# A tile's transposes between the halves of the tile before, and the input scaled on GpSimd: the first unit of a hybrid RG-LRU / mLSTM layer

## The chip, the cores and the metric

The kernel runs on one core of one Trainium2 chip. The metric is the time of one execution in device microseconds; the time of a kernel is the median of several runs. The engines are named as in the profile: PE (TensorE, the matrix products; PEld is its loading of weights), DVE (VectorE), ACT (ScalarE), POOL (GpSimd, which also issues the stores), SP (SyncE, which issues the loads).

## The reference, cut to what matters

One layer of a decoder trunk is computed for 1024 prompt tokens and for 8 single decode tokens. The part that the change touches is its start: a row-wise normalisation of the input and one wide input projection.

```
def rmsnorm(x, g):
    y = x * lax.rsqrt(jnp.mean(x * x, axis=-1, keepdims=True) + EPS)
    return y * g
...
hn = rmsnorm(x, g_norm)                 # x: 1024 tokens x 1024
u = hn @ w_in                           # 1024 x 7176
xa, za, uq, uk, uv, uo, zb, ui, uf = jnp.split(u, SPLIT_IDX, axis=-1)
...                                     # RG-LRU on xa, mLSTM on q, k, v, two gates, merge
x = x + merged @ w_out
y = rmsnorm(x, g_final)
```

The eight gate columns ui and uf are the last 8 of the 7176.

## The kernel before, in words

**Units.** The projection is done in 14 units of 512 columns (two blocks of 256). Units 1 to 13 use seven block products in place of eight (a Strassen-like scheme): they need the turned, normalised input and five sums and differences of its quarters, kept in SBUF as seven pairs cb_hi[q], cb_lo[q]. Every operand is split into a rounded high part and the low rest, and a product is the sum of three: high x high, high x low, low x high (mm3, L64 to L66). A split (L70, L71) is one cast on ACT (hi) and one subtraction on DVE (lo).

**The first unit** (v0 and v1, with the eight gate columns beside v0) is different: it does the plain product tile by tile of 128 tokens while the input arrives, and builds the seven pairs on the way. The change lies here. For each tile, in the order xorder = 4, 0, 8, 5, 1, 6, 2, 7, 3 (8 is the tile of the 8 decode tokens), the steps are:

- x_fetch (L366): load 128 x 1024 of x from SP's queue into a buffer of the pool ws, which has six and also holds the four tiles of split v1 weights w1h, w1l.
- x_stats (L371, L181 to L189): ACT squares the tile and sums it (tile junk), then the square root on ACT (L185) and four small steps on DVE give the factor in st.
- x_turn (L382, L386): one DVE operation multiplies x by the factor and by g_norm (gn_b); eight PE transposes put the turned tile into two PSUM banks (two of ps_kv, or ps_s and ps_qp, in turn).
- x_split (L70, L71): the two halves are cast and subtracted into b12h, b12l (tiles 4 to 7, first half) or into cb_hi, cb_lo.
- plain (L64 to L66): two halves of 24 products each, the first with the v0 weights and gates (wph, wpl), the second with the v1 weights (w1h, w1l), into ps_o, of which there are three banks. Each result is copied out by ACT (pe, L461) and stored by POOL (d_v, L464).
- x_copy and x_combos (L408, L420, L424 to L426): the sums and differences, each split again.

Ahead of the first tile 17 products of ones (L469) run on PE. Behind the last tile in the text come the gate product of the decode tokens (L510, bias added into gd, L512), the decode product of the first unit (dec_unit, L228: hnd against the raw weights) and the loads of the next unit's raw weights (raw_1, L215).

**What sets the order.** The text gives dependences and a priority; a scheduler places the instructions on each engine, and each engine then runs its queue in that order. So the order below is the built program's and not the text's.

Of the kernel before, what the change touches and what calls it, by code (L numbers as in the profile page):

```python
# [17 lines left out]
P = 128  # L18
T = 1024
HT = 512  # L20
NB = 8
KC = 8
# [27 lines left out]
def hymba_kernel(  # L50
# [7 lines left out]
    V, A, G, TE = nc.vector, nc.scalar, nc.gpsimd, nc.tensor  # L58
    ld = nc.sync.dma_start
    stq = nc.gpsimd.dma_start  # L60

    def mm3(out, ah, al, bh, bl, first, last):

        TE.matmul(out, ah, bh, start=first, stop=False, skip_group_check=True)  # L64
        TE.matmul(out, ah, bl, start=False, stop=False, skip_group_check=True)  # L65
        TE.matmul(out, al, bh, start=False, stop=last, skip_group_check=True)  # L66

    def split(hi, lo, src):

        A.copy(hi, src)  # L70
        V.tensor_tensor(lo, src, hi.bitcast(F32), op=ALU.subtract)  # L71
# [9 lines left out]
    def ps(tag, shape):  # L81
        return psp.tile(shape, F32, tag=tag, name=f"ps_{tag}", bufs=NBUF.get(tag, 1))
# [121 lines left out]
    raws = {}  # L204
# [18 lines left out]
    def dec_unit(u):  # L223

        pz = ps("tr", [P, 512])
        for k in range(KC):
            g = k % 4
            TE.matmul(pz[32 * g:32 * g + 32, :], hnd[:, k, :], raws[u, k // 4][:, k % 4, :], start=k < 4, stop=k >= 4,  # L228
                      skip_group_check=True)
# [12 lines left out]
        late.append(turn)  # L242
# [114 lines left out]
    es_f = ExitStack()  # L357
    fp = es_f.enter_context(tc.tile_pool(name="f_start", bufs=1))
    gn_b = fp.tile([P, T], F32, tag="gn_b", name="gn_b")
    xorder = [4, 0, 8, 5, 1, 6, 2, 7, 3]  # L360
    rows_of = lambda i: P if i < 8 else NB
    xt, xps, bf = {}, {}, {}

    def x_fetch(i):
        xt[i] = ws([P, T], f"x{i}", F32)
        ld(xt[i][:rows_of(i)], x_prompt[0, i * P:(i + 1) * P, :] if i < 8 else x_sample[:, 0, :])  # L366

    def x_stats(i):
        n = rows_of(i)
        junk = fp.tile([P, T], BF16, tag="junk", name="junk")  # L370
        A.activation(junk[:n], xt[i][:n], AF.Square, accum_out=st0[:n, i, 0:1])  # L371
        rsqrt_mean(st0[:n, i, 1:2], st0[:n, i, 0:1], st0[:n, i, 2:3], T)

    def x_turn(m):
        i = xorder[m]
        n = rows_of(i)
        xps[i] = []
        for half in range(2):
            hs = slice(half * HT, (half + 1) * HT)
            if m == 0 or half == 0:  # L380
                s = hs if m == 0 else slice(0, T)
                V.scalar_tensor_tensor(xt[i][:n, s], xt[i][:n, s], st0[:n, i, 1:2], gn_b[:n, s], op0=ALU.mult, op1=ALU.mult)  # L382
            pt = ps(("kv", "kv", "s", "qp")[(2 * m + half) % 4], [P, 4, P])
            for q in range(4):
                k = half * 4 + q
                TE.transpose(pt[:, q, 0:n], xt[i][:n, k * P:(k + 1) * P], idF[:n, :n])  # L386
            xps[i].append(pt)
        del xt[i]

    def x_split(i, half):  # L390

        p = xps[i][half]
        if i == 8:
            V.tensor_copy(hnd[:, 4 * half:4 * half + 4, 0:NB], p[:, :, 0:NB])
            return
        s = slice(i % 4 * P, (i % 4 + 1) * P)
        if i >= 4 and half == 0:
            bf[i] = [fp.tile([P, 4, P], F32R, tag=f"b12{n}", name=f"b12{n}") for n in "hl"]
            split(*bf[i], p)
        else:  # L400
            q = Q_P3 if i >= 4 else (Q_P1, Q_P2)[half]
            split(cb[q][0][:, :, s], cb[q][1][:, :, s], p)
# [33 lines left out]
    def w1_split(b):  # L436

        t = ws([P, 4, 256], f"w1h{b}"), ws([P, 4, 256], f"w1l{b}")
        split(t[0], t[1], raws[0, b][:, :, 256:512])
        w1.append(t)  # L440

    gs = dconst([P, NCH, 8], "gs")

    def plain(i):

        s = slice(i % 4 * P, (i % 4 + 1) * P)
        op = []
        for k in range(KC):
            if i < 4:
                op.append([t[:, k % 4, s] for t in cb[Q_P1 if k < 4 else Q_P2]])  # L450
            elif k < 4:
                op.append([t[:, k, :] for t in bf[i]])
            else:
                op.append([t[:, k % 4, s] for t in cb[Q_P3]])
        for w in range(2):
            pt = ps("o", [P, 512])[:, 0:264 - 8 * w]
            for k, (h, l) in enumerate(op):
                wh, wl = (hi[:, k, :], lo[:, k, :]) if w == 0 else (t[:, k % 4, :] for t in w1[k // 4])
                mm3(pt, h, l, wh, wl, k == 0, k == KC - 1)
            t = fp.tile([P, 256], F32, tag="pe", name="pe", bufs=2)  # L460
            A.copy(t, pt[:, 0:256])  # L461
            if w == 0:
                V.tensor_tensor(gs[:, i, :], pt[:, 256:264], bgate, op=ALU.add)
            stq(d_v[w][i * P:(i + 1) * P, :], t)  # L464

    pw = ps("tr", [P, P])

    for _ in range(17):
        TE.matmul(pw, ones, ones, start=True, stop=True)  # L469
    x_fetch(xorder[0])  # L470
    ld(gn_b, g_norm[0].partition_broadcast(P))
    load_raw(0, 0, (0,))
    ld(wg, w_in[0, :, C_G:C_G + 8].rearrange("(k p) c -> p k c", p=P))
    load_raw(0, 1, (0,))
    x_fetch(xorder[1])
    load_raw(0, 0, (1,))
    load_raw(0, 1, (1,))
    ld(bgate[:, 0:4], b_mi[0].partition_broadcast(P))
    ld(bgate[:, 4:8], b_mf[0].partition_broadcast(P))
    x_stats(xorder[0])  # L480
    x_stats(xorder[1])
    for m, i in enumerate(xorder):
        x_turn(m)
        if m == 0:
            def w0_split(k):
                split(hi[:, k:k + 2, 0:256], lo[:, k:k + 2, 0:256], raws[0, k // 4][:, k % 4:k % 4 + 2, 0:256])
            w0_split(0)
            split(hi[:, :, 256:264], lo[:, :, 256:264], wg)
            x_split(i, 0)
            w0_split(2)  # L490
            x_split(i, 1)
            w0_split(4)
            w0_split(6)
            for b in range(2):
                w1_split(b)
        else:
            x_split(i, 0)
            x_split(i, 1)
        if 4 <= i < 8:
            x_copy(i)  # L500
        if m + 2 < 9:
            x_fetch(xorder[m + 2])
            x_stats(xorder[m + 2])
        if i < 8:
            plain(i)
            x_combos(i)

    pgd = ps("tr", [32, 8])
    for k in range(KC):
        TE.matmul(pgd, hnd[:, k, :], wg[:, k, :], start=k == 0, stop=k == KC - 1)  # L510
    gd = dconst([NB, 8], "gd")
    V.tensor_tensor(gd, pgd[0:NB], bgate[0:NB], op=ALU.add)  # L512
    ld(d_gd, gd)
    dec_unit(0)
    load_raw(1, 0)
    load_raw(1, 1)
    es_f.close()


# [1021 lines left out]
```

## Time and profile before

| what | value |
|---|---|
| median of 3 runs | 948.93 us (947.85 to 950.67) |
| the profiled execution | 948.28 us, its span 946.5 us |
| PE busy | 927.4 us, 98% of the span |
| DVE, ACT, POOL busy | 75%, 62%, 15% |
| chain that ended last | PE 89%, DVE 5%, DMA 2%, ACT 2% |
| from the first product of the first unit to the first of the next | 9.80 to 79.24 us |

A row of the timeline reads: start, duration, engine, line, operation, output<-inputs, partitions x elements, and in brackets the idle time just before with what ended it. A row of the waits reads: who waited, for whom, total us, times, longest. PE's durations are those of a pipeline: products follow each other faster than one of them lasts, so work is read from start to start.

### The profile page before, as it was taken

To read this page: it belongs to the slowest core of one execution; us is meant where nothing else is said; L and a number is where in the kernel's file an instruction comes from. 1 tells how busy PE (TensorE), PEld (TensorE's weight loads), DVE (VectorE), ACT (ScalarE), POOL (GpSimd) and SP (SyncE) were. 2 spreads that over 40 slices of the span, in tenths; PEclk is the share of its full clock that TensorE was granted. 3 is DMA by queue.
4 is the path that set the end of the run, shared out by engine and by line. 5 is a ranking of instruction groups with operands and counts; after the bars stand their busy time and mean duration, and the time that the engine had idled before them with its cause. 6 is when DMAs were issued, how large, how long until landed. Compare 5 with 4: busy or idle time off the path is not lost.

```text
span 946.5 us, 15380 instructions
## 1 busy us (share of the span) xinstructions
PE 927.4 (98%) x5355; PEld 763.1 (81%) x5355; DVE 711.1 (75%) x1488; ACT 583.2 (62%) x1041; POOL 144.6 (15%) x254
## 2 busy tenths in 40 slices
PE   7999999999999999999999999999999999999996
PEld 7887778777787887777789898877687888888886
DVE  5876787889788788798877966678766777677663
ACT  5563446777677666768667684457646456456542
POOL 1110111121202131112112212010200100000110
PEclk9999999999999999999999999999999999999999
DMA  5431455275636564437645545436873664465431
GB/s 183 151 128 37 142 176 183 81 242 187 221 116 223 178 219 150 150 112 264 202 152 180 201 134 166 129 106 228 305 210 116 177 187 121 137 187 152 128 85 51
DMA packets 131251, 153.69 MB, mean 162 GB/s; under 512 B 15658, under 2 KB 109930, under 8 KB 131166
## 3 DMA queue, kind: packets, MB, share of 16 engines
q1 hardware_dynamic: 113446, 96.84, 34.5%
q0 software_dynamic: 17728, 55.87, 16.2%
q8 instruction: 42, 0.69, 0.3%
q14 instruction: 35, 0.29, 0.1%
HBM read 101.09 MB, written 51.65 MB: 161 GB/s over the span
## 4 chain that ended last, share of the span: by engine, by line
PE 89%; DVE 5%; DMA 2%; ACT 2%; issue 1%; SPq 0%; DVEq 0%; ACTq 0%
PE ps_o L64 14%; PE ps_o L66 14%; PE ps_o L65 14%; PE ps_kv L64 11%; PE ps_kv L65 10%; PE ps_kv L66 10%; PE ps_tr L228 3%; PE ps_s L746 2%; PE ps_s L1076 1%; PE ps_qp L910 1%; DMA raw<-in_w_in_dram 1%; PE ps_qp L64 1%; PE ps_tr L1213 1%; PE ps_qp L65 1%; PE ps_qp L66 1%
## 5 line engine op out<-in xcount | busy, mean ns | idle before, releaser
L70 ACT CAST wh<-raw 128x1024 fp32r<-128x1024 f32 x91 | 95.6, 1050 | 75.2 <-PE ps_o L65 30.3
L71 DVE TENSOR_TENSOR wl<-raw,wh 128x1024 fp32r<-128x1024 f32 x91 | 111.1, 1221 | 39.2 <-ACT wh L70 21.7
L64 PE MATMUL ps_kv<-cb_hi,wh 128*128 128x512 f32 x320 | 128.0, 400 | 0.7 <-ACT s L309 0.7
L66 PE MATMUL ps_kv<-cb_hi,wl 128*128 128x512 f32 x320 | 125.4, 392 | 0.0
L65 PE MATMUL ps_kv<-cb_lo,wh 128*128 128x512 f32 x320 | 125.1, 391 | 0.0
L64 PE MATMUL ps_o<-cb_hi,wh 128*128 128x512 f32 x240 | 94.8, 395 | 0.0
L66 PE MATMUL ps_o<-cb_hi,wl 128*128 128x512 f32 x240 | 93.7, 390 | 0.0
L65 PE MATMUL ps_o<-cb_lo,wh 128*128 128x512 f32 x240 | 93.6, 390 | 0.0
L64 PEld LDWEIGHTS ps_kv<-cb_hi,wh 128*128 128x128 f32 x320 | 60.1, 188 | 22.9 <-issue 5.5
L66 PEld LDWEIGHTS ps_kv<-cb_hi,wl 128*128 128x128 f32 x320 | 60.1, 188 | 13.1
L65 PEld LDWEIGHTS ps_kv<-cb_lo,wh 128*128 128x128 f32 x320 | 60.1, 188 | 11.8
L64 PE MATMUL ps_kv<-wh,cb_hi 128*128 128x256 f32 x192 | 55.1, 287 | 0.0
L65 PE MATMUL ps_kv<-wl,cb_hi 128*128 128x256 f32 x192 | 54.6, 284 | 0.0
L66 PE MATMUL ps_kv<-wh,cb_lo 128*128 128x256 f32 x192 | 54.5, 284 | 0.0
L64 PEld LDWEIGHTS ps_o<-cb_hi,wh 128*128 128x128 f32 x240 | 45.1, 188 | 11.6 <-issue 2.5
L64 PE MATMUL ps_o<-wo,mh 128*128 128x512 f32 (+1 forms) x136 | 53.2, 392 | 1.0 <-ACT mh L70 1.0
L66 PEld LDWEIGHTS ps_o<-cb_hi,wl 128*128 128x128 f32 x240 | 45.0, 188 | 9.8
L64 PE MATMUL ps_o<-wo,rh 128*128 128x512 f32 (+1 forms) x136 | 52.9, 389 | 0.0
L65 PEld LDWEIGHTS ps_o<-cb_lo,wh 128*128 128x128 f32 x240 | 45.1, 188 | 9.1
L66 PE MATMUL ps_o<-wo,rl 128*128 128x512 f32 (+1 forms) x136 | 51.8, 381 | 0.0
L65 PE MATMUL ps_o<-wo,rh 128*128 128x512 f32 (+1 forms) x136 | 51.7, 380 | 0.0
L65 PE MATMUL ps_o<-wo,mh 128*128 128x512 f32 (+1 forms) x136 | 51.6, 380 | 0.0
(469 smaller groups left out, 2524.9 us busy)
## 6 DMA issues: line engine op xcount, KB each, us to landing
raw<-in_w_in_dram SPq DMA_DIRECT2D x56, 512.0 KB
Cb<-in_state_mlstm_C_dram SPq DMA_DIRECT2D x32, 256.0 KB
out_dram<-Cb POOLq DMA_DIRECT2D x32, 256.0 KB, 4.1
qk<-d_qk SPq DMA_DIRECT2D x32, 256.0 KB
oraw<-in_w_out_dram SPq DMA_DIRECT2D x16, 512.0 KB
d_qk<-s POOLq DMA_DIRECT2D x24, 256.0 KB, 3.0
x<-in_x_prompt_dram SPq DMA_DIRECT2D x8, 512.0 KB
d_x<-s POOLq DMA_DIRECT2D x16, 256.0 KB, 2.5
```

Of the source, the lines that this page charges most:

```text
L64: TE.matmul(out, ah, bh, start=first, stop=False, skip_group_check=True)
L65: TE.matmul(out, ah, bl, start=False, stop=False, skip_group_check=True)
L66: TE.matmul(out, al, bh, start=False, stop=last, skip_group_check=True)
L70: A.copy(hi, src)
L71: V.tensor_tensor(lo, src, hi.bitcast(F32), op=ALU.subtract)
L228: TE.matmul(pz[32 * g:32 * g + 32, :], hnd[:, k, :], raws[u, k // 4][:, k % 4, :], start=k < 4, stop=k >= 4, skip_group_check=True)
L746: TE.matmul(pg, w[:, n, :], st["xx"][n], start=k == 0, stop=k == 1)
L910: TE.matmul(pq[32 * g:32 * g + n, 0:256], qsel[:, kb, 4 * bb:4 * bb + n], ds_["C", h * NB + bb][:, kb, :], start=b == 1, stop=b == NB - 1, ...
L1076: TE.matmul(S, qk[:, 2 + kb, :], qk[:, kb, :], start=kb == 0, stop=kb == 1)
L1213: TE.matmul(dec_o[0][32 * g:32 * g + 32, :], md, oraw[m][:, half * 512:(half + 1) * 512], start=first and m in ms[:2], stop=last and m in ...
```

## The change

All edits are in the first unit.

- The decode tile 8 leaves xorder; loads have an order of their own, xload, with the decode tile third. x_turn8 turns the decode tile into one bank ps_tr.
- x is scaled by two GpSimd operations in x_stats, a multiply by gn_b and a multiply by the factor, for all tiles but the first, which stays with DVE in x_turn. Every third tile loaded has a buffer x2 of its own; junk moves to the staging pool.
- plain does one half at a time, and its products are grouped by four: high x high, then low x high, then high x low (in the very first group high x low comes second). The next tile's transposes and splits stand between the two halves.
- The splits of the second weights and the statistics of the next tiles stand ahead of the first product; the copies b12f and b22f of the first tile stand behind its products.
- 19 and 4 products of ones instead of 17; the gate product, dec_unit(0) and the raw_1 loads stand behind the third tile.

Three places in the built programs. First PE, at the end of the first tile (x4, whose second half goes into ps_o_306 before and ps_o_338 now) and the transposes of the second tile, x0. Before:

```order
L66 MATMUL ps_o_306<-w1h1_259,cb_lo5_166 128x256
L386 MATMUL ps_s_339<-idF_78,x0_205 128x128 x4
L386 MATMUL ps_qp_344<-idF_78,x0_205 128x128 x4
L64 MATMUL ps_o_363<-wph_175,cb_hi0_155 128x264
L65 MATMUL ps_o_363<-wpl_176,cb_hi0_155 128x264
```

And now:

```order
L473 MATMUL ps_o_338<-w1h0_255,b12h_243 128x256 x4
L473 MATMUL ps_o_338<-w1h0_255,b12l_244 128x256 x2
L394 MATMUL ps_s_312<-idF_78,x0_207 128x128 x4
L394 MATMUL ps_qp_317<-idF_78,x0_207 128x128 x4
L473 MATMUL ps_o_338<-w1h0_255,b12l_244 128x256 x2
L473 MATMUL ps_o_338<-w1l0_256,b12h_243 128x256 x4
L473 MATMUL ps_o_338<-w1h1_269,cb_hi5_165 128x256 x4
L473 MATMUL ps_o_338<-w1h1_269,cb_lo5_166 128x256 x4
L473 MATMUL ps_o_338<-w1l1_270,cb_hi5_165 128x256 x4
L473 MATMUL ps_o_374<-wph_175,cb_hi0_155 128x264 x4
```

x0's transposes have moved from behind the tile's 48th product to behind its 30th; 18 products of the first tile now stand between them and the first product of x0. At x5 the transposes stand behind the 42nd product of x0, at x1 behind the 34th of x5, from x6 on behind the 24th.

Second POOL, from its last early instruction on (pe is the copied result of a half). Before, only stores are queued:

```order
L658 DMA out_8_dram<-in_state_rglru_conv_dram 8x2048
L464 DMA d_v0_129<-pe_302 128x256
L464 DMA d_v1_130<-pe_331 128x256
L464 DMA d_v0_129<-pe_388 128x256
L464 DMA d_v1_130<-pe_417 128x256
```

And now the two multiplies of each tile stand between the stores:

```order
L381 TENSOR_TENSOR x0_207<-x0_207,gn_b_174 128x1024
L479 DMA d_v0_129<-pe_308 128x256
L382 TENSOR_SCALAR x0_207<-x0_207,st0_117 128x1024
L381 TENSOR_TENSOR x8_213<-x8_213,gn_b_174 8x1024
L479 DMA d_v1_130<-pe_363 128x256
L382 TENSOR_SCALAR x8_213<-x8_213,st0_117 8x1024
L381 TENSOR_TENSOR x5_326<-x5_326,gn_b_174 128x1024
L479 DMA d_v0_129<-pe_399 128x256
L382 TENSOR_SCALAR x5_326<-x5_326,st0_117 128x1024
L381 TENSOR_TENSOR x1_429<-x1_429,gn_b_174 128x1024
L479 DMA d_v1_130<-pe_468 128x256
L381 TENSOR_TENSOR x6_441<-x6_441,gn_b_174 128x1024
```

A store that waits for the end of a half (pe) now holds back the second multiply of a tile, and a multiply holds back stores.

Third ACT, from the last cast of the v0 weights on. Before:

```order
L70 CAST wph_175<-raw1_0_203 128x2x256 x2
L408 COPY b12f_263<-ps_kv_228 128x512
L371 ACTIVATE junk_219,st0_117<-x0_205 128x1024
L408 COPY b22f_264<-ps_kv_234 128x512
L185 ACTIVATE st0_117<-st0_117 128x1
L70 CAST w1h0_255<-raw0_0_200 128x1024
L461 COPY pe_302<-ps_o_277 128x256
L70 CAST w1h1_259<-raw1_0_203 128x1024
```

And now:

```order
L70 CAST wph_175<-raw1_0_205 128x2x256 x2
L378 ACTIVATE junk_259,st0_117<-x0_207 128x1024
L185 ACTIVATE st0_117<-st0_117 128x1
L476 COPY pe_308<-ps_o_283 128x256
L70 CAST w1h0_255<-raw0_0_202 128x1024
L70 CAST w1h1_269<-raw1_0_205 128x1024
L70 CAST cb_hi0_155<-ps_s_312 128x4x128
```

The two copies of the first tile have left the place ahead of the second weights, and the copy pe of its first half, which stood behind the first of their casts, stands ahead of both.

The diff, cut to its core:

```diff
-    xorder = [4, 0, 8, 5, 1, 6, 2, 7, 3]
+    xorder = [4, 0, 5, 1, 6, 2, 7, 3]
+    xload = [4, 0, 8, 5, 1, 6, 2, 7, 3]
...
+    def x_fetch(n):
+        if n < len(xload):
+            i = xload[n]
+            xt[i] = fp.tile([P, T], F32, tag="x2", name=f"x{i}") if n % 3 == 2 else ws([P, T], f"x{i}", F32)
+            ld(xt[i][:rows_of(i)], x_prompt[0, i * P:(i + 1) * P, :] if i < 8 else x_sample[:, 0, :])
+    def x_stats(n, scale=True):
+        if n < len(xload):
+            i = xload[n]
+            r = rows_of(i)
+            junk = sg([P, T], "junk", BF16)
+            x = xt[i][:r]
+            A.activation(junk[:r], x, AF.Square, accum_out=st0[:r, i, 0:1])
+            rsqrt_mean(st0[:r, i, 1:2], st0[:r, i, 0:1], st0[:r, i, 2:3], T)
+            if scale:
+                G.tensor_tensor(x, x, gn_b[:r], op=ALU.mult)
+                G.tensor_scalar(x, x, st0[:r, i, 1:2], None, op0=ALU.mult)
...
-            if m == 0 or half == 0:
-                s = hs if m == 0 else slice(0, T)
-                V.scalar_tensor_tensor(xt[i][:n, s], xt[i][:n, s], st0[:n, i, 1:2], gn_b[:n, s], op0=ALU.mult, op1=ALU.mult)
+            if m == 0:
+                hs = slice(half * HT, (half + 1) * HT)
+                V.scalar_tensor_tensor(xt[i][:, hs], xt[i][:, hs], st0[:, i, 1:2], gn_b[:, hs], op0=ALU.mult, op1=ALU.mult)
...
+    def x_turn8():
+        pt = ps("tr", [P, KC, NB])
+        for k in range(KC):
+            TE.transpose(pt[:, k, :], xt[8][:NB, k * P:(k + 1) * P], idF[:NB, :NB])
+        V.tensor_copy(hnd[:, :, 0:0 + NB], pt)
+        del xt[8]
...
-    def plain(i):
+    def plain(i, w):
...
-        for w in range(2):
-            pt = ps("o", [P, 512])[:, 0:264 - 8 * w]
-            for k, (h, l) in enumerate(op):
-                wh, wl = (hi[:, k, :], lo[:, k, :]) if w == 0 else (t[:, k % 4, :] for t in w1[k // 4])
-                mm3(pt, h, l, wh, wl, k == 0, k == KC - 1)
+        pt = ps("o", [P, 512])[:, 0:264 - 8 * w]
+        for k0 in (0, 4):
+            terms = [(0, 0), (0, 1), (1, 0)] if w == 0 and i == xorder[0] and k0 == 0 else [(0, 0), (1, 0), (0, 1)]
+            for x, y in terms:
+                for k in range(k0, k0 + 4):
+                    wt = (hi, lo)[y][:, k, :] if w == 0 else w1[k // 4][y][:, k % 4, :]
+                    TE.matmul(pt, op[k][x], wt, start=k == 0 and (x, y) == (0, 0), stop=k == KC - 1 and (x, y) == terms[-1],
+                              skip_group_check=True)
...
-    for _ in range(17):
+    for _ in range(19):
...
+    x_fetch(2)
+    x_stats(0, False)
+    x_turn(0)
+    for _ in range(4):
+        TE.matmul(pw, ones, ones, start=True, stop=True)
...
+    w0_split(6)
+    w1_split(0)
+    x_stats(1)
+    w1_split(1)
+    x_stats(2)
     for m, i in enumerate(xorder):
+        plain(i, 0)
+        if m + 1 < 8:
+            x_turn(m + 1)
+            for half in range(2):
+                x_split(xorder[m + 1], half)
+        if m == 1:
+            x_turn8()
         if m == 0:
+            x_fetch(3)
+            x_stats(3)
+        elif m == 1:
+            x_fetch(4)
+            x_stats(4)
+            x_fetch(5)
+        plain(i, 1)
+        if i >= 4:
             x_copy(i)
+        x_combos(i)
+        if m == 1:
+            x_stats(5)
+        elif m > 1:
+            x_fetch(m + 4)
+            x_stats(m + 4)
+        if m == 2:
+            pgd = ps("tr", [32, 8])
...
+            dec_unit(0)
+            load_raw(1, 0)
+            load_raw(1, 1)
```

More of the change, by code (lines that the diff above doesn't have):

```diff
@@ L385, in x_turn @@
                 k = half * 4 + q
-                TE.transpose(pt[:, q, 0:n], xt[i][:n, k * P:(k + 1) * P], idF[:n, :n])
+                TE.transpose(pt[:, q, :], xt[i][:, k * P:(k + 1) * P], idF)
             xps[i].append(pt)
         del xt[i]
+    def x_turn8():
[4 more added lines that the diff above has]
+        del xt[8]
     def x_split(i, half):
         p = xps[i][half]
-        if i == 8:
-            V.tensor_copy(hnd[:, 4 * half:4 * half + 4, 0:NB], p[:, :, 0:NB])
-            return
         s = slice(i % 4 * P, (i % 4 + 1) * P)
@@ L454, in plain @@
                 op.append([t[:, k % 4, s] for t in cb[Q_P3]])
-        for w in range(2):
-            pt = ps("o", [P, 512])[:, 0:264 - 8 * w]
-            for k, (h, l) in enumerate(op):
-                wh, wl = (hi[:, k, :], lo[:, k, :]) if w == 0 else (t[:, k % 4, :] for t in w1[k // 4])
-                mm3(pt, h, l, wh, wl, k == 0, k == KC - 1)
[L460 to L464, printed above, removed]
+        pt = ps("o", [P, 512])[:, 0:264 - 8 * w]
[6 more added lines that the diff above has]
+                              skip_group_check=True)
+        t = fp.tile([P, 256], F32, tag="pe", name="pe", bufs=2)
+        A.copy(t, pt[:, 0:256])
+        if w == 0:
+            V.tensor_tensor(gs[:, i, :], pt[:, 256:264], bgate, op=ALU.add)
+        stq(d_v[w][i * P:(i + 1) * P, :], t)
     pw = ps("tr", [P, P])
-    for _ in range(17):
+    for _ in range(19):
         TE.matmul(pw, ones, ones, start=True, stop=True)
-    x_fetch(xorder[0])
+    x_fetch(0)
     ld(gn_b, g_norm[0].partition_broadcast(P))
@@ L474, in hymba_kernel @@
     load_raw(0, 1, (0,))
-    x_fetch(xorder[1])
+    x_fetch(1)
     load_raw(0, 0, (1,))
@@ L479, in hymba_kernel @@
     ld(bgate[:, 4:8], b_mf[0].partition_broadcast(P))
-    x_stats(xorder[0])
-    x_stats(xorder[1])
-    for m, i in enumerate(xorder):
-        x_turn(m)
-        if m == 0:
[L485 to L499, printed above, removed]
-            x_copy(i)
[L501 to L516, printed above, removed]
+    x_fetch(2)
[3 more added lines that the diff above has]
+        TE.matmul(pw, ones, ones, start=True, stop=True)
+    def w0_split(k):
+        split(hi[:, k:k + 2, 0:256], lo[:, k:k + 2, 0:256], raws[0, k // 4][:, k % 4:k % 4 + 2, 0:256])
@@ new lines, in hymba_kernel @@
+    w0_split(0)
+    split(hi[:, :, 256:264], lo[:, :, 256:264], wg)
+    x_split(xorder[0], 0)
+    w0_split(2)
+    x_split(xorder[0], 1)
+    w0_split(4)
+    w0_split(6)
[3 more added lines that the diff above has]
+    x_stats(2)
+    for m, i in enumerate(xorder):
+        plain(i, 0)
[5 more added lines that the diff above has]
+            x_turn8()
+        if m == 0:
+            x_fetch(3)
[6 more added lines that the diff above has]
+        if i >= 4:
+            x_copy(i)
+        x_combos(i)
[6 more added lines that the diff above has]
+            pgd = ps("tr", [32, 8])
+            for k in range(KC):
+                TE.matmul(pgd, hnd[:, k, :], wg[:, k, :], start=k == 0, stop=k == KC - 1)
+            gd = dconst([NB, 8], "gd")
+            V.tensor_tensor(gd, pgd[0:NB], bgate[0:NB], op=ALU.add)
+            ld(d_gd, gd)
+            dec_unit(0)
+            load_raw(1, 0)
+            load_raw(1, 1)
```

10 lines of the change are left out of this document (removed).

## The prediction

> **What bounds the kernel now.** I read the page first, then the busy time by stretch.
>
> ```profile
> span 946.5 us, 15380 instructions
> ...
> PE 927.4 (98%) x5355; PEld 763.1 (81%) x5355; DVE 711.1 (75%) x1488; ACT 583.2 (62%) x1041; POOL 144.6 (15%) x254
> ...
> 0.00:130.00 130.00, 121.43 (x774) 101.55 (x775) 91.24 (x222) 65.69 (x128) 16.75 (x40) 0.99 0.40 128
> 130.00:946.50 816.50, 805.99 (x4583) 661.59 (x4581) 619.82 (x1267) 517.46 (x913) 127.84 (x214) 1.00 0.53 168
> ```
>
> TensorE (PE, the first busy column) is the bound almost everywhere: 10.5 us of its idle time lie in the last 816.5 us, 8.6 us in the first 130 us, and all edits of the change lie in the first 80. A microsecond that PE gains or loses there moves the end by as much, as long as the rest stays PE-bound. I therefore price that stage on PE alone, from its first product to the first product of the next unit. The first five rows are from the timeline of PE (start, duration, work), the other two from the chain that ended last:
>
> ```profile
> 9.80 0.39 PE L64 MATMUL ps_o<-wph,b12h 128*128 128x264 f32 x1 [1.00 <-ACT b12h L70]
> ...
> 40.93 0.39 PE L64 MATMUL ps_o<-wph,cb_hi 128*128 128x264 f32 x1
> ...
> 46.82 0.60 PE L386 MATMUL ps_s<-idF,x 128*128 128x128 f32 x4
> ...
> 47.79 1.06 PE L228 MATMUL ps_tr<-raw,hnd 128*32 128x512 f32 x6
> 48.78 0.39 PE L64 MATMUL ps_o<-wph,b12h 128*128 128x264 f32 x1
> ...
> 77.39 1.85 PE ps_tr L228 x16
> 79.24 0.43 PE ps_kv L64
> ```
>
> The stage lasts 79.24 - 9.80 = 69.4 us. Tile x1 shows undisturbed work: 48 products from 40.93 to 46.82, 5.89 us (0.122 each), eight transposes in 0.97 (to 47.79), and one piece of the decode product (L228) in 0.99 (to 48.78). The next unit's decode product, in one piece, takes 1.85. The small items, and the other two pieces of the first decode product:
>
> ```profile
> 28.38 0.66 PE L386 MATMUL ps_kv<-idF,x 8*128 8x8 f32 x8
> 29.61 0.67 PE L510 MATMUL ps_tr<-wg,hnd 128*32 128x8 f32 x16 [0.57 <-DVE hnd L394]
> ...
> 32.10 1.04 PE L228 MATMUL ps_tr<-raw,hnd 128*32 128x512 f32 x2
> ...
> 39.93 1.06 PE L228 MATMUL ps_tr<-raw,hnd 128*32 128x512 f32 x8
> ```
>
> Work before: 8 x 5.89 + 7 x 0.97 + 0.66 + 0.67 + 3 x 0.99 + 1.85 = 60.1 us. So 9.3 us of the stage are lost. Whom PE waited for, from the view of waits (total, times, longest; the first 130 us):
>
> ```profile
> PE ps_o L64 <- ACT cb_hi L70: 1.3, 2, 1.1
> ...
> PE ps_o L66 <- DVE cb_lo L71: 0.9, 1, 0.9
> PE ps_o L65 <- DVE w1l L71: 0.9, 1, 0.9
> PE ps_s L386 <- DVE gd L512: 0.8, 1, 0.8
> PE ps_tr L510 <- DVE hnd L394: 0.6, 1, 0.6
> PE ps_o L64 <- ACT w1h L70: 0.6, 1, 0.6
> PE ps_o L66 <- DVE b12l L71: 0.5, 1, 0.5
> PE ps_s L386 <- ACT cb_hi L70: 0.5, 1, 0.5
> ```
>
> That is 6.1 us, nearly all at the seams between tiles, where the casts (ACT) and subtractions (VectorE, DVE) of fresh transposes end last. A further loss is the clock. In the one-microsecond stretch below the last three columns are granted clock, DMA share and GB/s; the other two rows are from PE's timeline:
>
> ```profile
> 17.00:18.00 1.00, 1.00 (x7) 1.00 (x6) 1.00 (x2) 0.00 (x0) 0.00 (x0) 0.50 0.00 0
> ...
> 16.42 0.42 PE L64 MATMUL ps_o<-w1h,b12h 128*128 128x256 f32 x1
> ...
> 19.62 0.33 PE L64 MATMUL ps_o<-w1h,cb_hi 128*128 128x256 f32 x1
> ```
>
> After the waits around 14 us PE runs at half clock: 15 products in 3.2 us instead of 15 x 0.122 = 1.8, a loss of 1.4. The last 1.8 us I put down to pipeline fills behind each wait.
>
> **The change, part by part.** *Decode product in one piece:* 3 x 0.99 becomes 1.85, a gain of 1.1, so the work after is 58.9 us.
>
> *Warm-up, and second weights.* PE, ACT and VectorE around the first tile:
>
> ```profile
> 1.14 6.39 PE L469 MATMUL ps_tr<-ones 128*128 128x128 f32 x34 [1.14 <-POOL ones L115]
> ...
> 9.17 0.57 ACT L70 CAST b12h<-ps_kv 128x512 fp32r<-128x512 f32 x1
> ...
> 11.17 0.59 ACT L408 COPY b12f<-ps_kv 128x512 f32<-128x512 f32 x1
> 11.65 1.07 ACT L371 ACTIVATE junk<-x 128x1024 bf16<-128x1024 f32 x1
> ...
> 13.27 1.05 ACT L70 CAST w1h<-raw 128x1024 fp32r<-128x1024 f32 x1
> 14.21 0.39 ACT L461 COPY pe<-ps_o 128x256 f32<-128x256 f32 x1
> ...
> 11.31 1.28 DVE L71 TENSOR_TENSOR wpl<-raw,wph 128x512 fp32r<-128x512 f32 x2
> ...
> L71 DVE TENSOR_TENSOR w1l<-raw,w1h 128x1024 fp32r<-128x1024 f32 x2 | 2.4, 1220 | 0.0
> ```
>
> Seventeen warm-up products took 6.39 us, 0.38 each. Six more in front of the transposes would end at 7.53 + 2.3 = 9.8 at worst, with the first half turned at 10.3, 1.1 behind the b12h cast of 9.17; nothing is lost if the later ones run faster, as a rising clock would have it. I take 0.3.
>
> The copies b12f and b22f leave the place ahead of the cast w1h, but the copy pe comes ahead of it, and pe waits for the first half to end. With its new order of terms that half waits for b12l no more, but its last products need the second wpl of 12.6: it ends at about 12.9. So junk runs from 11.2 to 12.2, pe from 13.1 to 13.4, w1h from 13.4 to 14.4, and PE idles 1.5 us, as much as it waited for w1h and w1l together before. Gain here: none. What pe holds up behind it on ACT is both w1h casts.
>
> *Transposes between the halves.* From tile x6 on, 24 products (2.9 us) stand between a tile's transposes and their first use; two casts (0.57 each, from the b12h row) and two subtractions (0.64, half the wpl row) need 2.4. The waits on cb_hi, cb_lo, hnd and gd go. Behind x5's transposes stand only six products, 0.7 us, and x8's tiny transposes are ahead of that: I keep 0.3 us. The loads of x rise in SP's queue; raw_1's first load falls behind x7's, and the rest of the stage hides it, since it is first cast near the stage's end.
>
> *Scaling on GpSimd.* The nearest rows:
>
> ```profile
> L382 DVE SCALAR_TENSOR_TENSOR x<-x,st,gn_b 128x1024 f32<-128x1024 f32 x7 | 9.0, 1284 | 0.2
> ...
> L115 POOL MEMSET ones<- 128x128 f32 x1 | 0.2, 205 | 0.0
> ...
> L147 POOL MEMSET hnd<- 128x256 f32 x1 | 0.3, 302 | 0.0
> masks.py:199 POOL TENSOR_SCALAR_AFFINE_SELECT idF<-idF 128x128 f32<-128x128 f32 x1 | 0.3, 289 | 0.0
> ...
> L464 POOL DMA_DIRECT2D d_v<-pe x16 | 8.7, 545 | 67.0 <-ACT pe L461 61.2 <-ACT st L185 5.8
> ```
>
> VectorE loses the seven operations of 1.28 us and x8's; that buys nothing by itself, beyond the seams. GpSimd gains two passes per tile, which no row shows. The memsets give (302 - 205) / 128 = 0.76 ns an element, so 0.9 us for 1024 that are only written; eight affine selects, which read and write, take 2.3, and two inputs could double that. Bounds: 0.9 to 4.6 us for the multiply by g, 0.9 to 2.3 for the one by the statistic. I take 2.3 for the first (reading twice, it is nearer the select) and 1.1 for the second (nearer the memset; ACT's pass over the same 1024 elements takes 1.07).
>
> The Trainium skill (GPSIMD Engine Reference, section 3.1) gives 4497 ns for a two-input add of 2048 elements; half of it, 2.25 us as an estimate, would leave the sum as it is.
>
> GpSimd's queue now alternates: multiply by g, store d_v (0.54, waiting for pe), multiply by the statistic. For x0: junk ends at 12.2, the first pass at 14.5, the store at 15.0, the second at 16.1. PE has six products from 14.4 to 15.1, then idles 1.0. With gaps again between 13 and 16 it should get the half clock again: 1.4, as before. x8 and x5 then pass in turn behind two stores, and x5 is ready some 0.7 us after PE wants it. x1's second pass stands behind x6's first: 0.4 to 1.5 late, I take 1.0. From there GpSimd needs 2.3 + 1.1 + 2 x 0.54 = 4.5 us a tile against PE's 5.89 + 0.97 = 6.9, and is ahead.
>
> *Sum:* 58.9 + 0.3 (warm-up) + 1.5 (w1h) + 1.0 (x0) + 1.4 (clock) + 0.7 (x5) + 1.0 (x1) + 0.3 (x5's casts) = 65.1 us against 69.4, a gain of 4.3. The profiled execution took 948.28 us (its span 946.5); it lies 0.65 below the median of the three runs. 948.3 - 4.3 = **944.0 us**.
>
> **The rivals.** *1. VectorE and GpSimd block each other.* Both work through SBUF at the same time for the first time here. Suppose that a VectorE operation with two SBUF inputs waits for a running GpSimd pass, and the other way round. Then x0's last statistics wait for the first pass to end and w1l (1.22) gets ahead of the second: x0 1.3 later. x5's statistics: 0.6. x5's low halves stand behind subtractions that wait for x1's pass: 1.6. The gate product: 0.6. A second half-clock stretch: 1.4. Together 5.5 us, 949.5. For it: VectorE is 75% busy, so the two will often meet. Against: no row shows such a wait.
>
> The Trainium skill (SBUF — State Buffer, "Who interferes with whom") states just this: a VectorE instruction with two SBUF inputs and a GpSimd instruction that reads SBUF exclude each other for their whole length. It speaks against the change, and no row of this trace bears on it.
>
> *2. GpSimd feeds too late, and the kernel is slower.* If the second pass takes the select's 2.3 us, 1.2 more each, on top of rival 1, x0 is 1.2 later, x5 2.0 (x8's passes lie ahead of it) and x1 1.2: 949.5 + 4.4 = 953.9. It decides once the two passes together exceed about 3.4 us with blocking, 4.5 without. For it: two inputs and no measured row. Against: the memsets' rate.
>
> *3. GpSimd at the memset's rate.* At 0.9 + 0.9 the waits for x0, x5 and x1 (2.7) go, and perhaps the slow clock (1.4): 939.9 us.
>
> *4. The seams do not close,* because ACT's casts queue behind junk and pe. ACT is 62% busy; a junk of 1.07 ahead of one cast fits into the half microsecond of cover left at most once or twice: under 1 us, inside the ranges.
>
> **How the numbers follow.** About 0.3%, 2.8 us, is what a measurement of this kernel can tell from no change. Forecast (942 to 946) 0.42; rival 3 0.10; rival 1, inside 0.3%, 0.27; rival 2 0.21. So faster 0.52, same 0.27, slower 0.21. The range of 8 in 10 leaves out the outer parts of rivals 2 and 3: 939.5 to 952.5.
>
> **What would show it.** Right: the next unit's first ps_kv product (L64) at about 75 us; PE waits for GpSimd's x only at x0, x5 and x1; passes near 2.3 and 1.1 us; the wait for w1h still about 1.5; one piece of L228. Wrong: VectorE's two-input rows longer than now or preceded by waits for GpSimd (rival 1); PE waiting for x beyond x1 (rival 2); no wait for x at all (rival 3); any change after 130 us.

## The result, and the profile after

The changed kernel takes **957.25 us** (median of 4 runs, 956.24 to 959.31) against 948.91 for the kernel before (947.85 to 950.67): a ratio of 1.0089, 95% interval 1.0064 to 1.0113. The forecast was 944.0, the range ended at 952.5, and slower had a chance of 0.21. The profiled execution took 959.31 us, the slowest of the four, so its trace tells where the time goes better than how much. First its page, then its busy time by stretch:

```profile
span 957.5 us, 15415 instructions
...
PE 931.2 (97%) x5367; PEld 768.7 (80%) x5367; DVE 710.6 (74%) x1479; ACT 582.4 (61%) x1041; POOL 188.3 (20%) x270
```

```profile
0.00:130.00 130.00, 115.41 (x741) 101.77 (x742) 84.05 (x193) 61.70 (x119) 60.16 (x55) 0.93 0.35 117
130.00:957.50 827.50, 815.84 (x4628) 666.92 (x4626) 626.56 (x1287) 520.73 (x922) 128.12 (x215) 1.00 0.53 167
```

Behind 130 us PE idles 11.7 us, before 10.5: little has changed there. Ahead of it PE idles 14.6 us instead of 8.6 and its clock is 0.93 in the mean. Four stretches of 10 us show where (first column after the length: PE; third from the end: granted clock):

```profile
10.00:20.00 10.00, 4.43 (x31) 3.85 (x30) 8.96 (x16) 5.74 (x11) 6.59 (x3) 0.85 0.55 184
20.00:30.00 10.00, 8.26 (x56) 8.05 (x57) 4.52 (x10) 6.17 (x14) 6.19 (x4) 0.81 0.20 67
30.00:40.00 10.00, 8.37 (x60) 8.06 (x60) 8.31 (x19) 5.45 (x12) 8.65 (x6) 0.83 0.36 130
40.00:50.00 10.00, 5.74 (x34) 5.54 (x33) 6.29 (x13) 3.71 (x9) 10.00 (x4) 0.72 0.12 34
```

The stage of the first unit, from its first product to the first product of the next unit, on PE's timeline:

```profile
10.72 0.76 PE L473 MATMUL ps_o<-wph,b12h 128*128 128x264 f32 x4 [0.62 <-ACT b12h L70]
...
20.05 1.12 PE L394 MATMUL ps_s<-idF,x 128*128 128x128 f32 x4 [3.59 <-POOL x L382]
...
45.85 1.12 PE L394 MATMUL ps_s<-idF,x 128*128 128x128 f32 x4 [4.26 <-POOL x L382]
...
88.01 0.50 PE L64 MATMUL ps_kv<-cb_hi,wh 128*128 128x512 f32 x1
```

It lasts 88.01 - 10.72 = 77.3 us; before it was 69.4, predicted were 65.1. Of the 11.0 us by which this span is longer than the one before (957.5 against 946.5), 7.9 lie in the stage, 0.9 ahead of it and 2.2 behind. Whom PE waited for (the view of waits, first 130 us), and GpSimd's two passes (groups of POOL):

```profile
PE ps_s L394 <- POOL x L382: 7.8, 2, 4.3
PE ps_tr L401 <- POOL x L382: 1.7, 1, 1.7
PE ps_kv L394 <- POOL x L382: 1.6, 1, 1.6
PE ps_o L473 <- ACT w1h L70: 1.4, 1, 1.4
...
PE ps_o L473 <- ACT b12h L70: 0.6, 1, 0.6
```

```profile
L382 POOL TENSOR_SCALAR x<-x,st 128x1024 f32<-128x1024 f32 x7 | 21.5, 3067 | 0.7 <-DVE gs L478 0.3 <-DVE st L189 0.3
L381 POOL TENSOR_TENSOR x<-x,gn_b 128x1024 f32<-128x1024 f32 x7 | 17.3, 2475 | 13.0 <-ACT junk L378 13.0
...
L382 POOL TENSOR_SCALAR x<-x,st 8x1024 f32<-8x1024 f32 x1 | 2.8, 2835 | 0.0
```

The waits on casts and subtractions at the seams between tiles are gone, as forecast (the 0.6 for b12h lies ahead of the first product); in their place PE waits 11.1 us (7.8 + 1.7 + 1.6) for x0, x8, x5 and x1. The multiply by the statistic takes 2.83 us undisturbed and 3.07 in the mean, not 1.1.

There is a second thing to see, on VectorE. The first rows are from its groups, the next two from its timeline, the others from POOL's:

```profile
L71 DVE TENSOR_TENSOR cb_lo<-t,cb_hi 128x512 fp32r<-128x512 f32 x16 | 12.0, 758 | 2.4 <-ACT cb_hi L70 2.4
L187 DVE TENSOR_TENSOR st<-st 128x1 f32<-128x1 f32 x8 | 5.3, 658 | 0.1
...
L438 DVE TENSOR_TENSOR t<-ps_qp,t 128x512 f32<-128x512 f32 x4 | 2.7, 676 | 0.0
```

```profile
14.05 1.70 DVE L187 TENSOR_TENSOR st<-st 128x1 f32<-128x1 f32 x1
...
40.52 2.57 DVE L432 TENSOR_TENSOR t<-b22f,b12f 128x512 f32<-128x512 f32 x1 [0.15 <-ACT b22f L420]
```

```profile
13.36 2.37 POOL L381 TENSOR_TENSOR x<-x,gn_b 128x1024 f32<-128x1024 f32 x1 [10.41 <-ACT junk L378]
15.68 0.61 POOL L479 DMA_DIRECT2D d_v<-pe  x1
16.33 3.67 POOL L382 TENSOR_SCALAR x<-x,st 128x1024 f32<-128x1024 f32 x1
...
39.61 2.93 POOL L381 TENSOR_TENSOR x<-x,gn_b 128x1024 f32<-128x1024 f32 x1 [0.76 <-ACT junk L378]
42.52 3.27 POOL L382 TENSOR_SCALAR x<-x,st 128x1024 f32<-128x1024 f32 x1
```

L187 squares one column of statistics, in 0.16 us where GpSimd is idle (e11, below). Here it takes 0.66 in the mean; from 14.05 it lasts 1.70 and ends at 15.75, when GpSimd's pass ends (13.36 + 2.37 = 15.73). L432 at 40.52 ends 0.55 after the pass of 39.61 has ended. L438, which takes one of its inputs from PSUM, lasts 0.68 as before. GpSimd is lengthened too: x0's second pass lasts 3.67 instead of 2.83, while the w1l subtraction beside it (17.27 on VectorE's timeline) lasts 2.06 instead of 1.22. So the engines do block each other where VectorE reads two operands from SBUF: the mechanism of rival 1.

### The profile page after: what moved, and what is told of

Same layout as the page of the kernel before. It is cut to its first block, busy times and chain, and to the rows that moved or that the text cites. A ratio compares the mean times of both kernels' runs of the same rounds, so it can differ in the third digit from the quotient of the medians.

```text
span 957.5 us, 15415 instructions
## 1 busy us (share of the span) xinstructions
PE 931.2 (97%) x5367; PEld 768.7 (80%) x5367; DVE 710.6 (74%) x1479; ACT 582.4 (61%) x1041; POOL 188.3 (20%) x270
## 4 chain that ended last, share of the span: by engine, by line
PE 87%; DVE 5%; DMA 3%; POOL 2%; ACT 2%; issue 1%; SPq 0%; POOLq 0%; DVEq 0%; ACTq 0%
PE ps_o L64 13%; PE ps_o L66 13%; PE ps_o L65 12%; PE ps_kv L64 10%; PE ps_kv L66 10%; PE ps_kv L65 10%; PE ps_o L473 3%; PE ps_tr L228 3%; PE ps_s L778 2%; PE ps_s L1108 1%; POOL x L382 1%; PE ps_qp L942 1%; DMA raw<-in_w_in_dram 1%; DMA oraw<-in_w_out_dram 1%; PE ps_qp L64 1%
```

## The experiments

Theory A: GpSimd's passes are too long, x comes late. Theory B: VectorE and GpSimd block each other. Theory Q, which came up with the first results: the stores d_v, queued between GpSimd's passes, hold up ACT, which needs their buffers. Theory C: the new order is itself the loss. The experiments ran on several chips, each beside the kernel before, which took 949.3 to 950.0 there and 948.9 in the comparison above, the only one in which the changed kernel ran; so a difference of about 1 us between medians from different chips says nothing.

### Who scales, in either order

```diff
 e1_vector_scales (the changed kernel with)
-                G.tensor_tensor(x, x, gn_b[:r], op=ALU.mult)
-                G.tensor_scalar(x, x, st0[:r, i, 1:2], None, op0=ALU.mult)
+                V.scalar_tensor_tensor(x, x, st0[:r, i, 1:2], gn_b[:r], op0=ALU.mult, op1=ALU.mult)
 e5_before_pool_scales (the kernel before, in x_stats; its VectorE operation kept for x4 alone)
+        if i != xorder[0]:
+            G.tensor_tensor(xt[i][:n], xt[i][:n], gn_b[:n], op=ALU.mult)
+            G.tensor_scalar(xt[i][:n], xt[i][:n], st0[:n, i, 1:2], None, op0=ALU.mult)
```

> The changed kernel with x scaled by VectorE again, one operation of 1.28 us in the place of GpSimd's two; the rest of the new order stays. Theory A (GpSimd feeds x too late): PE's 11.1 us of waits for GpSimd's x go and most of the half clock with them, while VectorE gets its 9 us back; about 944, 5 us below the kernel before. Theory B (the two engines block each other): also about 944. Theory C (the new order is itself the loss, by its later w1h casts and the later first product): 949 or more, PE waiting for casts instead of for x.

> The kernel before, its order unchanged, with x scaled by GpSimd in two operations right behind the statistics (x4 apart, which VectorE scales in halves as before). With e1 (new order, VectorE) this closes the square: if GpSimd's scaling costs the same in either order, 949.4 + 16.6 = 966; if the old order hides more of it, 955 to 960, since a tile lasts PE longer there; if GpSimd's scaling only hurts where transposes are early, 949 to 951.

| | VectorE scales | GpSimd scales |
|---|---|---|
| old order | 949 to 950 | 970.4 (ratio 1.0217, 1.0191 to 1.0244) |
| new order | 940.7 (0.9904, 0.9889 to 0.9919) | 957.3 |

The new order gains 9 us by itself, more than the 5 expected; theory C is out. GpSimd's scaling costs 16.6 us in the new order and 20.5 in the old, more than any of the three expectations for e5; perhaps the early transposes hide some of it, which was not tested. The stage of e1, on PE's timeline, and undisturbed pieces of its chain:

```profile
10.61 0.76 PE L473 MATMUL ps_o<-wph,b12h 128*128 128x264 f32 x4 [0.24 <-ACT b12h L70]
...
71.94 0.50 PE L64 MATMUL ps_kv<-cb_hi,wh 128*128 128x512 f32 x1
```

```profile
40.68 0.87 PE ps_kv L394 x8
41.55 5.78 PE ps_o L473 x48
```

It lasts 61.3 us. Work: 8 x 5.78 + 7 x 0.87 + 0.66 + 0.67 + 2 x 1.85 = 57.4 (the small items as in the prediction; the second decode product is in one piece too). So e1 loses 3.9 us, the changed kernel 19.9. From 10 to 50 us, where the changed kernel's clock stands at 0.72 to 0.85, e1's is 1.00 in each stretch of 10 us (view of windows).

### Blocking and queue, with nobody waiting for the results

e2 is e1 with GpSimd's passes on data that nobody reads (their scratch tile is PT in the rows). e8 and e11 are e2 and e1 with the stores issued by ACT.

```diff
 e2_vector_scales_pool_idle_work (e1 with)
+                for h in range(2):
+                    G.tensor_tensor(scr[:r], gn_b[:r, h * HT:(h + 1) * HT], gn_b[:r, h * HT:(h + 1) * HT], op=ALU.mult)
+                for h in range(2):
+                    G.tensor_scalar(scr[:r], gn_b[:r, h * HT:(h + 1) * HT], st0[:r, i, 1:2], None, op0=ALU.mult)
 e8, e9, e11, e12, e14 and e18 (in plain)
-        stq(d_v[w][i * P:(i + 1) * P, :], t)
+        nc.scalar.dma_start(d_v[w][i * P:(i + 1) * P, :], t)
```

> As e1_vector_scales, but GpSimd also does its passes at the same places (two halves of 512 elements each) from gn_b into a scratch tile that nobody reads, so that only contention is left. Theory A: equal to e1 within 1 us. Theory B: 4 to 6 us above e1, with VectorE's tiny statistics operation L187 and its two-SBUF-input subtractions lengthened (L187 from 0.16 to about 0.66 us in the mean). Half each: 2 to 3 us above e1.

> As e2_vector_scales_pool_idle_work, with the 16 stores d_v issued by ACT, right behind its copies pe, and no longer queued between GpSimd's passes. What is left of the extra 15 us of e2 against e1 is blocking between VectorE and GpSimd alone. Theory Q (the stores behind the passes hold up ACT, 9.1 us of waits of pe on d_v in e2): 943 to 946. Theory B (blocking): 951 or more, with VectorE's two-SBUF-input operations as long as in e2.

> Control for e8: e1_vector_scales with the stores d_v issued by ACT. ACT gets sixteen issues more; if one takes some 0.05 to 0.5 us there, the time stays within 2 us of e1's 940.7 by every theory.

Measured: e2 955.8, e8 947.6, e11 940.9. Theory B had given e2 4 to 6 us above e1. Of the 15.2 by which it is above, 8.2 go with the stores' place (e2 to e8) and 6.7 stay as blocking (e8 to e11); theories Q and B are both right. Part of the 6.7 lies ahead of the stage, where a first idle pass holds up x4's statistics, and the idle passes were rather longer than the real ones (1.57 us per half of 512 for the second), so it is no price of the changed kernel's own blocking. How the queue reaches ACT in e2, from ACT's timeline and POOL's:

```profile
50.32 0.37 ACT L481 COPY pe<-ps_o 128x256 f32<-128x256 f32 x1 [3.97 <-DMA d_v<-pe]
```

```profile
38.54 4.15 POOL L387 TENSOR_SCALAR PT<-gn_b,st 128x512 f32<-128x512 f32 x2
42.78 2.30 POOL L385 TENSOR_TENSOR PT<-gn_b 128x512 f32<-128x512 f32 x2
45.02 0.60 POOL L484 DMA_DIRECT2D d_v<-pe  x1
45.66 3.88 POOL L387 TENSOR_SCALAR PT<-gn_b,st 128x512 f32<-128x512 f32 x2
```

The store is issued at 45.02, behind two passes; the copy of 50.32 needs that buffer (pe has two) and had waited 3.97 us, with every cast queued behind it. Part of that wait is the store's own slow landing, some 5 us after its issue, where 2.1 is the median. In e8, where no store is in the way, blocking alone remains: L188 there is the operation that is L187 elsewhere, and takes 0.64 us in the mean against 0.16 in e11.

```profile
L188 DVE TENSOR_TENSOR st<-st 128x1 f32<-128x1 f32 x8 | 5.1, 643 | 0.2
```

```profile
L187 DVE TENSOR_TENSOR st<-st 128x1 f32<-128x1 f32 x8 | 1.3, 157 | 0.2
```

### The passes' length, and the stores, in the changed kernel

e10 shortens the second pass to about the price that the prediction had taken, by leaving 640 of the 1024 elements without the statistic; e7 gives it another form; e9 and e12 are the changed kernel and e10 with the stores on ACT.

```diff
 e10_second_pass_384
-                G.tensor_scalar(x, x, st0[:r, i, 1:2], None, op0=ALU.mult)
+                G.tensor_scalar(x[:, 0:384], x[:, 0:384], st0[:r, i, 1:2], None, op0=ALU.mult)
 e7_second_pass_tensor_tensor
+                G.tensor_tensor(x, x, st0[:r, i, 1:2].to_broadcast([r, T]), op=ALU.mult)
```

> The changed kernel with GpSimd's second pass over 384 of the 1024 elements only (the other 640 stay without the statistic), so that it takes about the 1.1 us that the prediction took for it. If the length of that pass is the whole error, the time comes out at the predicted 944. With blocking on top, as in rival 1, 949 to 951. If the length hardly matters, 955 or more.

> The changed kernel with the stores d_v issued by ACT instead of by GpSimd between its passes. Theory Q: 3 us or more below 957.3, since x0's second pass no longer stands behind a store that waits for pe (0.6 us each, and 0.3 us of wait), and no copy waits for a store. Theory B (blocking) and theory A (passes too long): 0.6 us earlier at x0, 1.2 at x5 and x1: 954 to 956.

> As e10_second_pass_384 (the second pass over 384 of 1024 elements, the rest stays without the statistic), with the stores d_v issued by ACT. It holds the price that the prediction took for that pass, and no store between the passes. If blocking is all that is left (e8 against e11: 6.7 us for somewhat longer passes), 946 to 948. If the stores were the rest of e10's 949.9, 944 or less.

> The changed kernel with GpSimd's second pass written as a two-input multiply with the statistic read with stride 0; the order on every engine stays the same. If the second pass then takes 2.37 us like the first instead of 2.84, theory A gives 0.5 less at x0, 1.0 at x5 (x8's pass lies ahead), 0.5 at x1: 957.3 - 2 = 955. Theory B: within 0.5 of the changed kernel. If the duration does not change, neither does the time.

| | median | 95% interval of the ratio to before |
|---|---|---|
| changed kernel | 957.3 | 1.0064 to 1.0113 |
| e7: second pass 1.88 us | 954.7 | 1.0028 to 1.0062 |
| e9: stores on ACT | 952.8 | 1.0020 to 1.0047 |
| e10: second pass 1.23 us | 949.9 | 0.9989 to 1.0016 |
| e12: both | 947.2 | 0.9961 to 0.9987 |

With the second pass at 1.23 us (undisturbed) the time is 949.9: 7.3 us less, and within 0.4 of the 949.5 that rival 1, blocking with passes of 2.3 and 1.1 us, had been priced at. But e10 changes more than a length. The transposes of a tile's second half need none of the 384 elements, so they wait for the first pass only, and at x0 and x1 they now come first. From PE's timeline of e10:

```profile
15.61 0.66 PE L394 MATMUL ps_qp<-idF,x 128*128 128x128 f32 x4 [1.83 <-POOL x L381]
```

So 7.3 us is not the price of the length alone, and that e10 met rival 1's figure is partly luck.

With the stores on ACT the time falls by 4.5 us, and by 2.8 behind a short pass. In the changed kernel this is not theory Q's wait for a buffer. Whom ACT waited for, in the changed kernel and in e2 (views of waits):

```profile
ACT pe L476 <- DMA d_v<-pe: 0.7, 1, 0.7
```

```profile
ACT pe L481 <- DMA d_v<-pe: 9.1, 3, 4.0
```

PE's waits for x0, x8 and x5 hardly change in e9 (4.0, 1.4 and 1.8 us, against 3.6, 1.7 and 1.6); x1's falls from 4.3 to 1.8. In the changed kernel x1's second pass, at 42.52, stands behind the first pass of x6 (39.61). In e9 it stands ahead of it, as POOL's timeline shows:

```profile
39.30 3.14 POOL L382 TENSOR_SCALAR x<-x,st 128x1024 f32<-128x1024 f32 x1 [1.88 <-DVE st L189]
42.41 2.39 POOL L381 TENSOR_TENSOR x<-x,gn_b 128x1024 f32<-128x1024 f32 x1
```

So most of what e9 gains seems to go with this changed order on GpSimd, which came with the stores' move; the order by itself was not tried.

e7 keeps all the transposes behind the second pass. It gained 2.6 where the length alone promised more (0.95 a pass instead of the 0.5 expected): its second pass, from POOL's groups, is shorter, but VectorE's L187 is held up longer than in the changed kernel (0.66 us):

```profile
L382 POOL TENSOR_TENSOR x<-x,st 128x1024 f32<-128x1024 f32 x7 | 14.4, 2058 | 2.3 <-DVE st L189 1.7 <-DVE gs L478 0.5
```

```profile
L187 DVE TENSOR_TENSOR st<-st 128x1 f32<-128x1 f32 x8 | 8.3, 1032 | 0.1
```

### Is it the second operand from SBUF?

e3 gives the second pass to ACT. e16 is e3, e15 the changed kernel, e18 e9 and e17 e1, each with the three small operations on the statistics written with one tensor operand and a per-partition scalar:

```diff
 e3_second_pass_on_act
-                G.tensor_scalar(x, x, st0[:r, i, 1:2], None, op0=ALU.mult)
+                A.mul(x, x, st0[:r, i, 1:2])
 e15, e16, e17, e18 (rsqrt_mean written out in x_stats; v, s, t are the three columns of st0)
-        V.tensor_tensor(t, out, out, op=ALU.mult)
-        V.scalar_tensor_tensor(t, t, -0.5, v, op0=ALU.mult, op1=ALU.mult)
-        V.scalar_tensor_tensor(out, t, 1.5, out, op0=ALU.add, op1=ALU.mult)
+            V.tensor_scalar(t, s, s, None, op0=ALU.mult)
+            V.tensor_scalar(t, t, -0.5, v, op0=ALU.mult, op1=ALU.mult)
+            V.tensor_scalar(s, t, 1.5, s, op0=ALU.add, op1=ALU.mult)
```

> The changed kernel with the multiply by the statistic on ACT (1.07 us, as its pass for the squares) and only the multiply by g on GpSimd. By length and blocking of the second pass: as e10 or a little better, 947 to 950, with VectorE's operations lengthened about half as often. If ACT's queue is too full for it, 952 or more, with PE waiting for ACT's casts.

> e3_second_pass_on_act with the same rewriting. ACT waited 6.9 us for st there, and PE 6.7 us for x. If the second operand is what blocks: 949 to 951 against e3's 955.3. If not: 954 to 956.

> The changed kernel with the three operations on st that read two SBUF tensors (one column each) written as tensor_scalar, the second factor as a per-partition scalar. If the second tensor operand is what GpSimd holds up, they take 0.15 us each again (L187 alone lost 4.0 us in the sum of eight); GpSimd's second passes hardly waited for st there (the stores stood before them), so only 0.5 to 2 us below 957.3. If any VectorE operation waits, the durations stay.

> e9_after_stores_on_act with the same rewriting. There GpSimd idled 6.5 us in all for st. If the second operand is what blocks: 949 to 951, against e9's 952.8, with that idle time gone. If not: 952 to 954.

> Control: e1_vector_scales with the same rewriting; GpSimd has no passes, so nothing is blocked: 940.7 within 1 us by every theory.

e3 missed its expectation: 955.3. Its VectorE, POOL and ACT, each from its timeline, around x8:

```profile
22.94 2.90 DVE L188 SCALAR_TENSOR_TENSOR st<-st 8x1 f32<-8x1 f32 x1
```

```profile
23.45 2.38 POOL L381 TENSOR_TENSOR x<-x,gn_b 128x1024 f32<-128x1024 f32 x1
```

```profile
26.12 1.15 ACT L382 ACTIVATE x<-x,st 8x1024 f32<-8x1024 f32 x1 [3.38 <-DVE st L181]
```

An operation on one column ends with GpSimd's pass, at 25.84, after 2.90 us, and ACT stands idle for 3.38 us, with all its casts behind it. In e16 the same operation takes 0.20 (VectorE's timeline), although GpSimd's passes are the same, and PE hardly waits for x any more (view of waits):

```profile
21.66 0.20 DVE L384 TENSOR_SCALAR st<-st 8x1 f32<-8x1 f32 x1
```

```profile
PE ps_o L479 <- DVE b12l L71: 1.9, 1, 1.9
PE ps_o L479 <- ACT b12h L70: 1.9, 3, 1.5
PE ps_o L479 <- ACT w1h L70: 1.4, 1, 1.4
...
PE ps_s L400 <- ACT x L388: 0.3, 1, 0.3
```

e16 takes 946.5 (0.9955 to 0.9985), 8.8 below e3 and lower than the 949 to 951 expected; the control e17 is at 940.0 against e1's 940.7. So it is the second operand from SBUF: the same arithmetic beside the same passes isn't held up when that factor is a per-partition scalar. In e15 (955.5) and e18 (952.5) the durations fell too, but little time: 1.7 us against the changed kernel, with intervals that overlap, and 0.3 against e9. In the changed kernel x0's statistics had ended at 16.13, before the store that stood ahead of the second pass (16.29), so nothing waited for them. For e18 the expectation of 949 to 951 was wrong, and the idle time of GpSimd before its second passes did not go. Its longest such wait, from POOL's timeline, and what it waited for, from VectorE's:

```profile
40.93 3.14 POOL L388 TENSOR_SCALAR x<-x,st 128x1024 f32<-128x1024 f32 x1 [3.44 <-DVE st L385]
```

```profile
40.55 0.21 DVE L385 TENSOR_SCALAR st<-st 128x1 f32<-128x1 f32 x1
```

That operation is short, so it isn't blocked; it and its two predecessors (38.46 and 39.83) stand in VectorE's queue among the subtractions that follow x5's transposes (the first at 37.00), and those had waited for x5 itself. What e16 has left against e1 stands in its waits on b12l and b12h, behind VectorE's subtractions of b22f and t, which stayed blocked.

### GpSimd for the late tiles only

```diff
-            if scale:
+            if scale and n < 5:
+                V.scalar_tensor_tensor(x, x, st0[:r, i, 1:2], gn_b[:r], op0=ALU.mult, op1=ALU.mult)
+            elif scale:
```

> VectorE scales x0, x8, x5 and x1, GpSimd keeps its two passes for x6, x2, x7 and x3, where PE did not wait for it. Theory A (only the first tiles' feed is late): all of the loss goes, 943 to 945, equal to e1 or 1 below it since VectorE has 5 us less to do. Theory B: e1 plus half of what e2 adds to e1.

> As e4_vector_scales_first_four (GpSimd scales x6, x2, x7 and x3 only) with the stores d_v issued by ACT. ACT's 4.2 us of waits for the stores go: 942 to 943 by theory Q with blocking of the four late tiles left (1 to 2 us above e11's 940.9); 945 or more if blocking alone makes e4's loss; at or below 940.5 if GpSimd's share does help VectorE.

Measured: 945.8 and 943.9. Taking GpSimd's hands off the four early tiles gives back 11.4 of the 16.6 us, about what PE had waited for x0, x8, x5 and x1 (11.1); but even where PE waits for none of its results, GpSimd costs 5.1 us against e1, and 3.0 against e11 with the stores moved. Its relief of VectorE bought nothing: e1, with 9 us more VectorE work in the stage, is the fastest form of the changed kernel, together with e17.

## Why the prediction was wrong

**The step that failed** is the price of the multiply by the statistic: "1.1 for the second (nearer the memset; ACT's pass over the same 1024 elements takes 1.07)". It takes 2.83, above even the upper bound of 2.3 that the affine select gave. The bounds were taken from rows that do other work: a pass that reads one tensor turned out dearer than one that reads two (2.37).

At x0 the step can be followed to the end. The second pass was to run from 15.0 to 16.1 and ran from 16.33 to 20.00; PE, which was to want x0 at 15.1, wanted it at 16.46. Everything ahead of the pass came some 1.3 us late for both, so the wait of 3.6 instead of 1.0 is the pass: 1.7 by its undisturbed length, 0.8 by the subtraction of w1l beside it. e7 shows the length's effect on the whole time in an experiment: 0.95 us less a pass, 2.6 us less in all. e10, with 1.6 less, took 7.3 off, but freed half of the transposes too.

**The second failure** is the forecast's assumption that the passes run beside VectorE at no cost. Rival 1 had the mechanism, and a chance of 0.27. The Trainium skill (SBUF — State Buffer, "Who interferes with whom") says that a VectorE instruction with two SBUF inputs contends with a GpSimd instruction that reads SBUF. By that rule e3's operations are held up and e16's, with one tensor operand, escape; the runs agree (2.90 against 0.20 us). The prediction's "for their whole length" held beside GpSimd's multiply of two tensors, and not always beside its multiply by the statistic (last section). Rival 1 had put 1.3 us on x0, by late statistics and by w1l ahead of the second pass. The statistics cost nothing there, since they ended at 16.13 and the store in front of the pass at 16.29; w1l, beside the pass, cost 0.8.

Rival 2, the one on the slower side, joined the two causes. 953.9 was 3.4 short: it took 2.3 for the pass and allowed for one more stretch of half clock only. Its sign, PE waiting for x beyond x1, did not show.

Point by point. *Without GpSimd's terms* the sum was 65.1 - 1.0 - 1.4 - 0.7 - 1.0 = 61.0 us for the stage; e1 measured 61.3. That they are so near is partly luck: the undisturbed work was 57.4 instead of 58.9, and e1 lost 3.9 us where 2.1 had been put, 0.3 of that for a warm-up that lies ahead of the stage. The seams, the decode product in one piece and the wait for w1h (1.41 us in e1, put at 1.5) came out as worked out. *GpSimd's terms* were 4.1 us and came to 77.3 - 61.3 = 16.0: x0 3.6 (put at 1.0), x8 1.7 (0), x5 1.6 (0.7), x1 4.3 (1.0), 11.1 in all for 2.7. Most of the rest is slow clock, put at 1.4: beside its waits for x and w1h (11.1 + 1.4) the changed kernel loses 19.9 - 12.5 = 7.4 us, while the clock stands at 0.72 to 0.85. *The multiply by g* at 2.3 was right (2.37). *The place* of the waits (x0, x5, x1) was right, x8 was missed. *The stores* were priced at 0.54 us each in GpSimd's queue, and one at 15.68 took 0.61; that moving them would be worth 4.5 us (e9), most of it at x1, was not seen.

How much of the 16.6 us belongs to each cause has no single answer, since they overlap and two of the experiments moved more than one thing. e10 gains 7.3, e9 4.5, both together 10.1. What then remains holds the length of the passes that are left, PE's waits for them, and blocking; the share of blocking in the changed kernel itself was not isolated.

## What to carry to other kernels

An idle engine isn't free capacity: before moving work to GpSimd, ask what it shares with VectorE, what its queue already carries (stores whose buffers another engine needs), and who waits for the result at the start of a stage, and take its price only from a row of the same operation. A chain of tiny operations beside the passes can be held up for a whole pass; written with per-partition scalars instead of second tensors, it wasn't (0.20 us against 2.90). And an experiment that shortens or moves one thing can reorder others: read its queues before pricing it. Where a change has two parts, try each without the other: here one was worth -9 us and the other +17.

## What the runs showed of the hardware

- GpSimd, 1024 elements a partition: multiply of two tensors 2.37 us; tensor_scalar with a per-partition factor 2.83; the same multiply as a tensor_tensor whose second operand has stride 0, 1.88. Eight partitions cost the same as 128 (the tensor_scalar took 2.83 us on eight).
- A TENSOR_TENSOR pass of GpSimd held a VectorE operation with two SBUF inputs to the pass's end when the operation began clearly inside it (14.05 and 40.52 above). Where both began together it went either way: in e16 a subtraction of 28.52 lasted 2.90 us beside a pass that ran from 28.50 to 30.86; in the changed kernel one of 39.62 took its usual 0.68, and the pass of 39.61 took 2.93 instead of 2.37.
- A TENSOR_SCALAR pass did not always hold it: in the changed kernel L187 began at 43.25 and lasted 0.82 us beside a pass that ran from 42.52 to 45.79.
- In e3 the L188 shown above began 0.51 us before the recorded start of the pass that it then waited for, while GpSimd was issuing a store (22.85, 0.58 us). In the changed kernel the same operation took its usual 0.15 us at 26.18, inside the issue of another store (26.09, 0.60 us), so an issue alone needn't hold it; what held it in e3 before the pass began stays open.
